# Hybrid attention block on one core: the softmax division moved to VectorE, the keys' second copies moved to DMA transfers

## The chip, the cores and the metric

The kernel runs on one core of a Trainium2 chip. The core has TensorE (PE in the profile; PEld is its weight loading), VectorE (DVE), ScalarE (ACT), GpSimd (POOL) and SyncE (SP), each with an instruction queue of its own that is worked off in order, and 16 DMA engines that serve transfers issued from the queues. The metric is the device time of one execution in microseconds (us). Before the change it is 976.67 us, the median of three runs (975.41, 976.67, 982.44).

## What is computed

One layer over 512 positions of width 2048, in float32. A modulated RMSNorm is followed by one wide input projection, then two token mixers read it: a dilated-window attention with 16 heads of 64, and a gated linear attention (GLA) with 4 heads. Both are gated, joined, projected out, added to the residual and normalised. Cut to the attention, which the change touches:

```python
s = jnp.einsum('bnqrhe,bnkrhe->bhrnqk', qb, kw) * (E ** -0.5)
s = s + bias[None, :, None, None]
s = jnp.where(mask, s, NEG_INF)
m = jnp.max(s, axis=-1, keepdims=True)
p = jnp.exp(s - m)
den = jnp.sum(p, axis=-1, keepdims=True)
o = jnp.einsum('bhrnqk,bnkrhe->bhrnqe', p / den, vw)
...
mix_w = jax.nn.softmax(jnp.stack(lses, axis=0), axis=0)
att = jnp.einsum('pbsh,pbshe->bshe', mix_w, jnp.stack(outs, axis=0))
```

The three dilation patterns share one softmax in the kernel: a row of biases per head holds the pattern multiplicities, so that one 512 by 512 score matrix per head gives the merged result.

## The kernel before, in words

**Precision.** Every large product is made of float32r matmuls of high and low parts: `three` (lines 168 to 171) multiplies high by high, low by high and high by low. Weights come in by transfers of 512 KB on SyncE's queue (`fetch`, L299) into four buffers, ScalarE rounds them to the high part (L326), VectorE subtracts to get the low part (L310).

**Units.** After a first part that computes the values and the first queries and keys (`sta`, `stb`), the projections run as units of 192 matmuls each: qk2, qk4, qk6 (queries and keys of two pairs of heads each), gk, gv0, gv1, ag0, ag1, gg0, gg1, o0 to o3. TensorE's order is the order of the code (it is scheduled by hand); the order on the other engines is set by the tile framework. Each unit takes a list of side work that is dropped in between its matmuls at given fractions of the unit (`unit`). Units qk2, qk4, qk6 and gk carry the attention of four heads each, that is 16 tiles of 128 queries by 512 keys (`attention`): 64 tiles in all. qk6 and gk carry sums as well: VectorE multiplies half matrices of 512 KB (`rawv`) with a broadcast row (`shb`) and adds them up (L698, L259).

**Queries and keys.** `qk_evict` (L549) takes a pair of heads out of PSUM at the end of a unit. For each head, 64 partitions `own` hold it and the other 64, `oth`, get a copy, so that one matmul over 128 partitions adds the query's high and low part against the same keys. The query's high part goes to `own` (ScalarE, L557), its low part to `oth` (VectorE, L558). The keys' high part `ks` is written by ScalarE twice, to `own` (L566) and to `oth` (L567); the keys' low part `kl` by VectorE twice (L568, L569).

**One tile of attention.** `score`: two matmuls of queries with `ks` and `kl` (L594, L595); VectorE adds the biases and finds the row's extreme (L598, to `p` and `st`); ScalarE takes the exponential with the row sum (L601); VectorE inverts the sum (L602, 128 by 1); GpSimd multiplies the tile by it (L603). `turn`, which stands after the next tile's `score` in TensorE's order: four transposes of the tile to PSUM (L615), ScalarE's rounded copy (L619) and VectorE's remainder (L620). `values`: eight matmuls with the values per two tiles (L629), then ScalarE and VectorE bring the output to `cat` (L632, L636).

GpSimd does nothing else until the GLA (L785) and the last projection (L1042). SyncE's queue carries the weight loads, the biases per head (L582) and the half matrices (L693).

Of the kernel before, what the change touches and what calls it, by code (L numbers as in the profile page):

```python
# [10 lines left out]
F32 = mybir.dt.float32  # L11
F32R = mybir.dt.float32r
I32 = mybir.dt.int32
AF = mybir.ActivationFunctionType
ALU = mybir.AluOpType
# [118 lines left out]
def block_kernel(ctx: ExitStack, tc: tile.TileContext, a: dict):  # L134
    nc = tc.nc
# [11 lines left out]
    def T2(name, dt=F32, parts=P):  # L147
        return t2.tile([parts, 512], dt, tag="t2", name=name)

    def B8(name, shape, dt=F32):  # L150
        return b8.tile([P] + shape, dt, tag="b8", name=name)
# [4 lines left out]
    def PA(name):  # L156
        return pp.tile([P, 512], F32, tag="pa", bufs=3, name=name)

    mm = nc.tensor.matmul
    tt = nc.vector.tensor_tensor  # L160
    stt = nc.vector.scalar_tensor_tensor
    act = nc.scalar.activation
# [335 lines left out]
    for i in range(n):  # L498
        mm_task(i)
        st, k, j = chain[i]  # L500
# [15 lines left out]
    for i in range(n, 2 * n):  # L516
        mm_task(i)
        st, k, j = chain[i]
# [30 lines left out]
    def qk_evict(p, psq, psk):  # L549

        for j in range(2):
            own = slice(64 * j, 64 * j + 64)
            oth = slice(64 - 64 * j, 128 - 64 * j)
            qs = T2(f"qs{p}{j}", F32R)
            act(qs[own], psq[own, ::-1], AF.Copy, scale=-0.125)  # L557
            stt(qs[oth], psq[own, ::-1], -0.125, qs[own].bitcast(F32),  # L558
                op0=ALU.mult, op1=ALU.subtract)
            stacks[2 * p + j] = [qs, None, None, own]  # L560
        for j in range(2):
            own = slice(64 * j, 64 * j + 64)
            oth = slice(64 - 64 * j, 128 - 64 * j)
            ks = T2(f"ks{p}{j}", F32R)
            kl = T2(f"kl{p}{j}", F32R)
            act(ks[own], psk[own], AF.Copy)  # L566
            act(ks[oth], psk[own], AF.Copy)  # L567
            tt(kl[own], psk[own], ks[own].bitcast(F32), op=ALU.subtract)  # L568
            tt(kl[oth], psk[own], ks[own].bitcast(F32), op=ALU.subtract)  # L569
            stacks[2 * p + j][1:3] = ks, kl  # L570

    cat = [None] * 4
# [1 line left out]
    def attention(pairs):  # L574

        tiles = [(2 * p + j, i) for p in pairs for j in range(2) for i in range(4)]
        gt, pt, pr_ = {}, {}, {}
        heads = [2 * p + j for p in pairs for j in range(2)]

        def g_load(h):  # L580
            g = gp.tile([P, 896], F32, tag="g", name=f"g{h}")
            nc.sync.dma_start(g, bass.AP(grow.tensor, grow.offset + h * 1024, [[1, P], [1, 896]]))  # L582
            gt[h] = g

        def score(h, i):
            def go():
                if h % 8 == 0 and i == 0:
                    cat[h // 8] = B8(f"cat{h // 8}", [4, 512])
                if i == 1 and h != heads[-1]:
                    g_load(h + 1)  # L590
                qs, ks, kl, _ = stacks[h]
                q = slice(P * i, P * i + P)
                ps = PA(f"s{h}{i}")
                mm(ps, qs[:, q], ks, start=True, stop=False)  # L594
                mm(ps, qs[:, q], kl, start=False, stop=True)  # L595
                t = T2(f"p{h}{i}")
                st = sm.tile([P, 3], F32, tag="st", name=f"st{h}{i}", bufs=6)
                nc.vector.tensor_tensor_reduce(  # L598
                    out=t, in0=ps, in1=gt[h][:, P * i:P * i + 512], op0=ALU.add, op1=ALU.min,
                    scale=1.0, scalar=3e38, accum_out=st[:, 0:1])  # L600
                act(t, t, AF.Exp, bias=st[:, 0:1], scale=-1.0, accum_out=st[:, 1:2])  # L601
                nc.vector.reciprocal(st[:, 2:3], st[:, 1:2])  # L602
                nc.gpsimd.tensor_scalar(t, t, st[:, 2:3], 1.0, op0=ALU.mult, op1=ALU.mult)  # L603
                pr_[h, i] = t
            return go

        def turn(h, i):
            def go():
                half, ii = divmod(i, 2)
                if ii == 0:  # L610
                    pt[h, half] = B8(f"pt{h}{half}", [2, 4, 256], F32R)
                t = pr_.pop((h, i))
                pk = PA(f"t{h}{i}")
                for kt in range(4):
                    nc.tensor.transpose(pk[:, kt * P:kt * P + P], t[:, kt * P:kt * P + P], ident)  # L615
                hi = pt[h, half][:, 0, :, P * ii:P * ii + P]
                lo = pt[h, half][:, 1, :, P * ii:P * ii + P]
                src = pk.rearrange("p (k q) -> p k q", k=4)
                act(hi, src, AF.Copy)  # L619
                tt(lo, src, hi.bitcast(F32), op=ALU.subtract)  # L620
            return go

        def values(h, half):
            def go():
                t = pt.pop((h, half))
                po = PA(f"o{h}{half}")
                for kt in range(4):
                    for w in range(2):
                        mm(po[:, :256], vv[h // 4][:, kt, h % 4, :], t[:, w, kt, :],  # L629
                           start=kt == 0 and w == 0, stop=kt == 3 and w == 1)  # L630
                oh = sm.tile([64, 256], F32, tag="oh", name=f"oh{h}{half}", bufs=1)
                act(oh, po[64:128, :256], AF.Copy)  # L632
                own = stacks[h][3]
                p = h // 2
                dst = cat[p // 4][own, p % 4, 256 - 256 * half:512 - 256 * half]
                tt(dst[:, ::-1], po[0:64, :256], oh, op=ALU.add)  # L636
            return go

        items = []
        n = len(tiles)  # L640
        for x in range(n + 3):
            if x < n:
                items.append(score(*tiles[x]))
            if 1 <= x <= n:
                items.append(turn(*tiles[x - 1]))
            if 2 <= x <= n + 1 and tiles[x - 2][1] % 2 == 1:
                items.append(values(tiles[x - 2][0], tiles[x - 2][1] // 2))
        g_load(heads[0])
        start, span, move0, move1, move_last = ATT_AT
        at = [start + (q + 0.5) / len(items) * span for q in range(len(items))]  # L650
        at[0] -= move0
        at[1] -= move1
        at[-1] += move_last
        return list(zip(at, items))
# [263 lines left out]
    for p in range(2):  # L918
        qk_evict(p, psb["b", 4 + 2 * p], psb["b", 5 + 2 * p])
    for n, p in (("qk2", 0), ("qk4", 2), ("qk6", 4)):  # L920
        ps = unit(n, False, attention((p, p + 1)) + ([(0.05, shift_row)] + some_sums(n) if p == 4 else []))
        for q in range(2):
            qk_evict(p + 2 + q, ps[2 * q], ps[2 * q + 1])
# [248 lines left out]
```

## Time and profile before

| | us |
|---|---|
| median of the runs, lowest, highest | 976.67, 975.41, 982.44 |
| span of the profiled execution | 976.7 |
| TensorE busy, idle in that span | 949.3, 27.4 |
| the stretch with attention, about | 200 to 478 |
| TensorE idle in that stretch | 12.3 |
| VectorE, ScalarE, GpSimd busy in that stretch | 186.1, 157.2, 46.4 |

The page gives no other time for the profiled execution than its span, which lies on the median. Its parts are: busy time per engine; the span in 40 slices; the DMA queues; the chain of work that ended last; groups of instructions by line, each with its count, busy time, mean duration and the idle time in front of it with what ended it; and the DMA transfers by line. Further views of the same trace list the waits of one engine, the busy time in chosen stretches, and the instructions in order of time (start, duration, engine, line, output and input, and in brackets the idle time before it with what ended it). The granted TensorE clock is 0.996 on average.

### The profile page before, as it was taken

The numbers are of one execution on the slowest core, as the hardware profiler recorded it, in microseconds if no ns is written. First come the engines' busy times: TensorE is split into PE (matmuls) and PEld (weight loads), VectorE is DVE, ScalarE is ACT, GpSimd is POOL, SyncE is SP. The second block draws the span as 40 slices with busy tenths as digits, with TensorE's granted clock in tenths as the row PEclk, the third lists the DMA queues.
The fourth block names the chain that finished last, engine by engine and source line by source line (L and its number), as shares of the span: only waits on it lengthen the run. The fifth ranks groups of instructions, "written<-read, shape, count | busy, mean of one in ns | idle before, by whom it ended". The sixth has DMA issues, their size and how long they took to land.

```text
span 976.7 us, 12006 instructions
## 1 busy us (share of the span) xinstructions
PE 949.3 (97%) x4522; PEld 782.3 (80%) x4522; DVE 619.8 (63%) x926; ACT 436.1 (45%) x731; POOL 77.4 (8%) x96
## 2 busy tenths in 40 slices
PE   8999999989999999999999999999999999999996
PEld 5888788878878777777777888888888888888886
DVE  7987899676666675776534647595885352436442
ACT  4542533565655655655413544363744151324221
POOL 0000000011111121111000000000010000203110
PEclk9999999999999999999999999999999999999998
DMA  9999487422223253432444434455465455345013
GB/s 328 411 413 369 158 324 274 132 99 77 93 84 101 86 192 103 127 107 91 135 169 162 130 108 142 139 170 176 130 220 181 141 173 192 106 132 171 22 43 130
DMA packets 42849, 159.69 MB, mean 163 GB/s; under 512 B 5252, under 2 KB 5796, under 8 KB 38056
## 3 DMA queue, kind: packets, MB, share of 16 engines
q1 hardware_dynamic: 42616, 158.61, 47.1%
q8 instruction: 35, 0.57, 0.2%
q10 hardware_dynamic: 176, 0.33, 0.1%
q14 instruction: 22, 0.18, 0.1%
HBM read 154.64 MB, written 4.28 MB: 163 GB/s over the span
## 4 chain that ended last, share of the span: by engine, by line
PE 76%; DVE 10%; DMA 5%; ACT 4%; issue 4%; POOL 1%; DVEq 0%; POOLq 0%; ACTq 0%
PE ps_o L170 6%; PE ps_o L169 6%; PE ps_o L171 6%; DMA rawg<-in_wg 4%; PE ps_qk L169 3%; PE sta L169 3%; PE stb L169 3%; PE ps_qk L171 3%; PE ps_qk L170 3%; PE stb L170 3%; PE sta L170 3%; PE stb L171 3%; PE sta L171 3%; PE ps_gv L171 3%; PE ps_gv L170 3%
## 5 line engine op out<-in xcount | busy, mean ns | idle before, releaser
L603 POOL TENSOR_SCALAR p<-p,st 128x512 f32<-128x512 f32 x64 | 46.4, 724 | 428.2 <-DVE st L602 412.7
L601 ACT ACTIVATE p<-p,st 128x512 f32<-128x512 f32 x64 | 46.1, 721 | 62.2 <-DVE st L598 62.1
L259 DVE CUSTOM_DVE_ANT_0 cb<-cb,sb,c_bcond 128x2048 f32<-128x2048 f32 (+1 forms) x32 | 73.4, 2293 | 0.1
L620 DVE TENSOR_TENSOR pt<-t,pt 128x512 fp32r<-128x512 f32 x64 | 44.1, 689 | 17.8 <-ACT pt L619 17.7
L615 PE MATMUL t<-c_ident,p 128*128 128x128 f32 x256 | 38.9, 274 | 10.0 <-POOL p L603 10.0
L615 PEld LDWEIGHTS t<-c_ident,p 128*128 128x128 f32 x256 | 30.9, 140 | 21.7 <-POOL p L603 14.9
L598 DVE CUSTOM_DVE_ANT_0 p<-s,g 128x512 f32<-128x512 f32 x64 | 43.6, 686 | 7.0 <-PE s L595 6.5
L619 ACT ACTIVATE pt<-t 128x512 fp32r<-128x512 f32 x64 | 37.9, 592 | 21.0 <-PE t L615 20.4
L259 DVE CUSTOM_DVE_ANT_0 rawg<-rawg,sb,gate 128x1024 f32<-128x1024 f32 x16 | 20.6, 1290 | 26.6 <-DMA rawg<-in_wg 26.6
L259 DVE CUSTOM_DVE_ANT_0 rawg<-rawg,sb,c_bcond 128x1024 f32<-128x1024 f32 x16 | 20.5, 1283 | 26.5 <-DMA rawg<-in_wg 26.5
L629 PEld LDWEIGHTS o<-pt,vv 128*128 128x128 f32 x256 | 34.2, 189 | 3.6 <-DVE pt L620 1.7
L629 PE MATMUL o<-pt,vv 128*128 128x256 f32 x256 | 35.9, 282 | 0.0
L1042 POOL TENSOR_TENSOR x<-x,fgain 128x512 f32<-128x512 f32 x12 | 20.3, 1697 | 184.6 <-ACT ysq L1032 184.6
L1032 ACT ACTIVATE ysq<-x 128x512 f32<-128x512 f32 (+1 forms) x17 | 10.3, 606 | 48.8 <-DVE x L1029 46.8
L602 DVE RECIPROCAL st<-st 128x1 f32<-128x1 f32 x64 | 10.4, 162 | 31.3 <-ACT p L601 31.2
L785 POOL TENSOR_SCALAR dc<-st,sc 128x256 f32<-128x256 f32 x16 | 10.5, 657 | 243.3 <-DVE st L782 238.4
L1028 DVE TENSOR_TENSOR y<-ps_o,sb 128x512 f32<-128x512 f32 (+1 forms) x17 | 11.1, 653 | 23.6 <-PE ps_o L171 23.6
L594 PE MATMUL s<-ks,qs 128*128 128x512 f32 x64 | 25.3, 396 | 0.2 <-DVE qs L558 0.2
L595 PE MATMUL s<-kl,qs 128*128 128x512 f32 x64 | 25.0, 390 | 0.0
L792 ACT ACTIVATE sq<-st,sc 128x256 f32<-128x256 f32 x24 | 12.2, 509 | 25.6 <-DVE st L787 13.5
L636 DVE TENSOR_TENSOR cat<-o,oh 64x256 f32<-64x256 f32 x32 | 13.3, 416 | 12.1 <-ACT oh L632 11.8
L632 ACT ACTIVATE oh<-o 64x256 f32<-64x256 f32 x32 | 12.2, 381 | 17.4 <-PE o L629 16.7
(1285 smaller groups left out, 2964.0 us busy)
## 6 DMA issues: line engine op xcount, KB each, us to landing
cb<-in_wm SPq DMA_DIRECT2D x31, 1024.0 KB, 10.0
rawg<-in_wg SPq DMA_DIRECT2D x32, 512.0 KB, 3.4
raw_o<-in_w_o SPq DMA_DIRECT2D x32, 512.0 KB, 3.5
raw_qk<-in_w_qk SPq DMA_DIRECT2D x24, 512.0 KB, 3.4
rawb<-in_w_sb SPq DMA_DIRECT2D x16, 512.0 KB, 5.8
rawv<-in_wv SPq DMA_DIRECT2D x16, 512.0 KB, 3.4
raw_gv<-in_w_gv SPq DMA_DIRECT2D x16, 512.0 KB, 3.4
raw_ag<-in_w_ag SPq DMA_DIRECT2D x16, 512.0 KB, 3.3
```

What stands on the lines that cost most here:

```text
L169: mm(ps, lh, rh, start=first, stop=False)
L170: mm(ps, ll, rh, start=False, stop=False)
L171: mm(ps, lh, rl, start=False, stop=last)
L259: nc.vector.tensor_tensor_reduce(out=w, in0=w, in1=with_, op0=ALU.mult, op1=ALU.add, scale=1.0, scalar=init, accum_out=dst)
L594: mm(ps, qs[:, q], ks, start=True, stop=False)
L598: nc.vector.tensor_tensor_reduce(out=t, in0=ps, in1=gt[h][:, P * i:P * i + 512], op0=ALU.add, op1=ALU.min, scale=1.0, scalar=3e38, accum_o ...
L601: act(t, t, AF.Exp, bias=st[:, 0:1], scale=-1.0, accum_out=st[:, 1:2])
L603: nc.gpsimd.tensor_scalar(t, t, st[:, 2:3], 1.0, op0=ALU.mult, op1=ALU.mult)
L615: nc.tensor.transpose(pk[:, kt * P:kt * P + P], t[:, kt * P:kt * P + P], ident)
L619: act(hi, src, AF.Copy)
L620: tt(lo, src, hi.bitcast(F32), op=ALU.subtract)
L629: mm(po[:, :256], vv[h // 4][:, kt, h % 4, :], t[:, w, kt, :], start=kt == 0 and w == 0, stop=kt == 3 and w == 1)
```

## The change

The division on L603 is issued on VectorE with one operation instead of on GpSimd with two (the second multiplied by 1.0). L567 and L569, which wrote the second copies of the keys' parts from PSUM on ScalarE and VectorE, become transfers from the first copy on GpSimd's queue, 64 partitions by 2 KB each. No buffer, no matmul and no position of side work is touched, and the order on TensorE and on SyncE's queue is the same row by row.

```diff
@@ qk_evict
             act(ks[own], psk[own], AF.Copy)
-            act(ks[oth], psk[own], AF.Copy)
+            nc.gpsimd.dma_start(ks[oth], ks[own])
             tt(kl[own], psk[own], ks[own].bitcast(F32), op=ALU.subtract)
-            tt(kl[oth], psk[own], ks[own].bitcast(F32), op=ALU.subtract)
+            nc.gpsimd.dma_start(kl[oth], kl[own])
             stacks[2 * p + j][1:3] = ks, kl
@@ score
                 nc.vector.reciprocal(st[:, 2:3], st[:, 1:2])
-                nc.gpsimd.tensor_scalar(t, t, st[:, 2:3], 1.0, op0=ALU.mult, op1=ALU.mult)
+                nc.vector.tensor_scalar(t, t, st[:, 2:3], None, op0=ALU.mult)
                 pr_[h, i] = t
```

How this moves the instructions stands in three places. First VectorE before the first attention tile, in unit qk2. `kl_1494` and `kl_1500` are the low keys of the second pair of heads, `qk23l` a weight's low part, `p_1551` and `p_1566` the first two tiles. Before:

```order
L568 TENSOR_TENSOR kl_1494<-stb_890,ks_1493 64x512
L569 TENSOR_TENSOR kl_1494<-stb_890,ks_1493 64x512
L310 TENSOR_TENSOR qk23l<-raw_qk_1513,qk23h 128x1024
L568 TENSOR_TENSOR kl_1500<-stb_890,ks_1499 64x512
L569 TENSOR_TENSOR kl_1500<-stb_890,ks_1499 64x512
L598 ISA p_1551,st_1552<-s_1548,g_1505 128x512
L598 ISA st_1552 128x1
L598 ISA p_1566,st_1567<-s_1563,g_1505 128x512
L598 ISA st_1567 128x1
L602 RECIPROCAL st_1552<-st_1552 128x1
L602 RECIPROCAL st_1567<-st_1567 128x1
L620 TENSOR_TENSOR pt_1587<-t_1588,pt_1587 128x4x128
```

After:

```order
L568 TENSOR_TENSOR kl_1494<-stb_890,ks_1493 64x512
L310 TENSOR_TENSOR qk23l<-raw_qk_1513,qk23h 128x1024
L568 TENSOR_TENSOR kl_1500<-stb_890,ks_1499 64x512
L598 ISA p_1551,st_1552<-s_1548,g_1505 128x512
L598 ISA st_1552 128x1
L598 ISA p_1566,st_1567<-s_1563,g_1505 128x512
L598 ISA st_1567 128x1
L602 RECIPROCAL st_1552<-st_1552 128x1
L603 TENSOR_SCALAR p_1551<-p_1551,st_1552 128x512
L602 RECIPROCAL st_1567<-st_1567 128x1
L603 TENSOR_SCALAR p_1566<-p_1566,st_1567 128x512
L620 TENSOR_TENSOR pt_1587<-t_1588,pt_1587 128x4x128
```

The second subtractions are gone from in front of the tile, and each division stands right behind its reciprocal.

Second, VectorE a little after the first tiles of unit qk6, where the first sums stand (`rawv_2818` and `rawv_2885`); `p_2911` is the unit's third tile, `pt_2897` takes the remainders of the first two. Before:

```order
L602 RECIPROCAL st_2874<-st_2874 128x1
L698 ISA rawv_2818,vbias_1468<-rawv_2818,shb 128x1024
L698 ISA vbias_1468 128x1
L620 TENSOR_TENSOR pt_2897<-t_2898,pt_2897 128x4x128
L598 ISA p_2911,st_2912<-s_2908,g_2788 128x512
L598 ISA st_2912 128x1
L259 ISA rawv_2885,vbias<-rawv_2885,shb,vbias_1468 128x1024
L259 ISA vbias 128x1
L602 RECIPROCAL st_2912<-st_2912 128x1
L310 TENSOR_TENSOR qk64l<-raw_qk_2849,qk64h 128x1024
L620 TENSOR_TENSOR pt_2897<-t_2925,pt_2897 128x4x128
```

After:

```order
L603 TENSOR_SCALAR p_2873<-p_2873,st_2874 128x512
L698 ISA rawv_2818,vbias_1468<-rawv_2818,shb 128x1024
L698 ISA vbias_1468 128x1
L259 ISA rawv_2885,vbias<-rawv_2885,shb,vbias_1468 128x1024
L259 ISA vbias 128x1
L620 TENSOR_TENSOR pt_2897<-t_2898,pt_2897 128x4x128
L598 ISA p_2911,st_2912<-s_2908,g_2788 128x512
L598 ISA st_2912 128x1
L310 TENSOR_TENSOR qk64l<-raw_qk_2849,qk64h 128x1024
L602 RECIPROCAL st_2912<-st_2912 128x1
L620 TENSOR_TENSOR pt_2897<-t_2925,pt_2897 128x4x128
L603 TENSOR_SCALAR p_2911<-p_2911,st_2912 128x512
```

The second sum has moved from behind the third tile's L598 to before it, and between that tile's reciprocal and its division the remainder of the tile before now stands.

Third, GpSimd's queue after the program's start. `ks_1475`, `kl_1476` are the keys of the first head, the others those of the next two. After the change:

```order
L567 DMA ks_1475<-ks_1475 64x512
L569 DMA kl_1476<-kl_1476 64x512
L567 DMA ks_1481<-ks_1481 64x512
L569 DMA kl_1482<-kl_1482 64x512
L567 DMA ks_1493<-ks_1493 64x512
L569 DMA kl_1494<-kl_1494 64x512
```

Where the 64 divisions stood, 32 transfers stand now, and the GLA's work (L785) follows behind the last of them.

## The prediction

> **What bounds the kernel now.** The first part of the page says which engine is full.
>
> ```profile
> PE 949.3 (97%) x4522; PEld 782.3 (80%) x4522; DVE 619.8 (63%) x926; ACT 436.1 (45%) x731; POOL 77.4 (8%) x96
> ```
>
> TensorE is busy for 949.3 of 976.7 us, in its own fixed order. The change adds and removes no matmul, so it can only move TensorE's 27.4 us of idle time. The busy time by stretch (columns: length, then busy time of PE, PEld, DVE, ACT, POOL, clock, DMA) shows how much of that lies where it acts, in units qk2, qk4, qk6 and gk.
>
> ```profile
> 200.00:261.00 61.00, 57.84 (x305) 47.94 (x305) 38.76 (x82) 34.00 (x67) 10.46 (x15) 1.00 0.26 84
> 261.00:331.00 70.00, 68.06 (x361) 56.33 (x361) 45.31 (x95) 40.62 (x79) 11.15 (x16) 1.00 0.28 88
> 331.00:402.00 71.00, 67.58 (x354) 55.22 (x353) 49.79 (x103) 39.78 (x78) 12.89 (x16) 1.00 0.42 137
> 402.00:478.00 76.00, 72.23 (x377) 59.11 (x376) 52.23 (x106) 42.78 (x83) 11.87 (x17) 1.00 0.37 118
> ```
>
> TensorE idles 3.16 + 1.94 + 3.42 + 3.77 = 12.3 us there. That is the ceiling of any gain, 1.3%. VectorE is 64% to 70% busy. What TensorE waited for (total, times, longest):
>
> ```profile
> PE t L615 <- POOL p L603: 10.0, 11, 2.9
> PE ps_qk L169 <- DVE qs L558: 1.0, 2, 0.5
> PE ps_gk L169 <- DVE qs L558: 0.5, 1, 0.5
> PE ps_qk L169 <- DVE kl L569: 0.2, 1, 0.2
> PE ps_gk L169 <- DVE kl L569: 0.2, 1, 0.2
> ```
>
> 10.0 us are transposes waiting for GpSimd's division, only 11 of 64 times. The other rows are a unit's first matmuls, which wait until VectorE has emptied a PSUM bank. In order of time the waits are of four kinds:
>
> ```profile
> 203.21 0.39 PE L595 MATMUL s<-kl,qs 128*128 128x512 f32 x1
> 204.50 0.47 PE L594 MATMUL s<-ks,qs 128*128 128x512 f32 x1 [0.22 <-DVE qs L558]
> 211.58 0.66 PE L615 MATMUL t<-c_ident,p 128*128 128x128 f32 x4 [2.94 <-POOL p L603]
> ...
> 263.83 0.66 PE L615 MATMUL t<-c_ident,p 128*128 128x128 f32 x4 [0.38 <-POOL p L603]
> ...
> 270.48 0.47 PE L169 MATMUL ps_qk<-h_hi,qk40h 128*128 128x512 f32 x1 [0.23 <-DVE kl L569]
> 272.61 0.47 PE L169 MATMUL ps_qk<-h_hi,qk40h 128*128 128x512 f32 x1 [0.52 <-DVE qs L558]
> 274.99 0.39 PE L595 MATMUL s<-kl,qs 128*128 128x512 f32 x1
> 280.71 0.66 PE L615 MATMUL t<-c_ident,p 128*128 128x128 f32 x4 [0.80 <-POOL p L603]
> ...
> 355.87 0.66 PE L615 MATMUL t<-c_ident,p 128*128 128x128 f32 x4 [0.19 <-POOL p L603]
> 371.00 0.66 PE L615 MATMUL t<-c_ident,p 128*128 128x128 f32 x4 [1.10 <-POOL p L603]
> ```
>
> At 204 to 212 and at 270 to 281 it is the start of a unit's attention, while the keys are still being evicted; at 263.83 a unit's last tile; at 355.87 and 371.00 tiles behind the sums. Why a tile is late, VectorE's rows before the first tile show, with GpSimd's first division:
>
> ```profile
> 198.22 0.68 DVE L568 TENSOR_TENSOR kl<-stb,ks 64x512 fp32r<-64x512 f32 x1 [0.53 <-ACT ks L567]
> 198.91 0.68 DVE L569 TENSOR_TENSOR kl<-stb,ks 64x512 fp32r<-64x512 f32 x1
> ...
> 204.88 0.68 DVE L568 TENSOR_TENSOR kl<-stb,ks 64x512 fp32r<-64x512 f32 x1 [0.52 <-ACT ks L567]
> 205.58 0.68 DVE L569 TENSOR_TENSOR kl<-stb,ks 64x512 fp32r<-64x512 f32 x1
> ...
> 208.99 0.69 DVE L598 CUSTOM_DVE_ANT_0 p<-s,g 128x512 f32<-128x512 f32 x1
> ...
> 210.57 0.16 DVE L602 RECIPROCAL st<-st 128x1 f32<-128x1 f32 x1 [0.27 <-ACT p L601]
> ...
> 264.60 0.68 DVE L568 TENSOR_TENSOR kl<-ps_qk,ks 64x512 fp32r<-64x512 f32 x1 [0.51 <-ACT ks L567]
> ```
>
> ```profile
> 210.83 1.40 POOL L603 TENSOR_SCALAR p<-p,st 128x512 f32<-128x512 f32 x2 [210.39 <-DVE st L602]
> ```
>
> The scores were done near 203.6, yet L598 starts at 208.99, because VectorE first works off the keys. So not the division's length but VectorE's queue sets the largest waits, and the two edits act on it in opposite directions.
>
> **The price of each edit.**
>
> ```profile
> L603 POOL TENSOR_SCALAR p<-p,st 128x512 f32<-128x512 f32 x64 | 46.4, 724 | 428.2 <-DVE st L602 412.7 <-PE ps_qk L171 5.1 <-DVE cat L636 4.4
> L569 DVE TENSOR_TENSOR kl<-ps_qk,ks 64x512 fp32r<-64x512 f32 x12 | 8.3, 689 | 0.2
> L567 ACT ACTIVATE ks<-ps_qk 64x512 fp32r<-64x512 f32 x12 | 7.1, 593 | 0.1
> ```
>
> The same operation, shape and form as the new division runs on VectorE at the end of the kernel (least, median, most ns):
>
> ```profile
> L1063 DVE TENSOR_SCALAR x<-x,rn x4: 479/480/483, 948.6 to 971.3; 128x512 f32<-128x512 f32 x4
> ```
>
> So VectorE gains 64 × 0.48 = 30.7 us and loses 16 × 0.69 = 11.0: net +19.7, from 186.1 to 205.8 us of about 272, or 76%. ScalarE loses 16 × 0.59 = 9.5. For a single tile the way from the reciprocal's end to the transposes shrinks: 0.48 and about 0.1 for two hand-overs, instead of 0.10 + 0.70 + 0.05 (reciprocal over at 210.73, GpSimd from 210.83, two divisions in 1.40, transposes at 211.58).
>
> *First entry (200 to 212).* Four second subtractions, 2.76, leave the queue before L598, and with them one of the 0.59 copies that the 0.53 and 0.52 waits stand for: L598 starts near 208.99 − 3.3 = 205.7. From L598 to the reciprocal's end it is 1.74 (210.73 − 208.99), plus 0.58 to the transposes: ready at 208.0. TensorE gets there at 211.58 − 2.94 − 0.22 = 208.4. Both waits go: −3.16. With the 2.76 alone it is ready at 208.55, and 0.15 stays.
>
> *The other three entries.* In each unit four subtractions (2.76) and four copies leave the eviction. The waits of 0.23 and 0.52 end more than 1 us earlier, and L598 of the unit's first tile comes at least 2 us earlier, against 0.80 that is missing. All go: 1.5 of L558, 0.4 of L569, and three waits of 0.80 for the division: −4.3.
>
> *Late tiles in the middle (371.00 and its like in gk).* VectorE's rows in qk6:
>
> ```profile
> 349.82 0.16 DVE L602 RECIPROCAL st<-st 128x1 f32<-128x1 f32 x1 [0.54 <-ACT p L601]
> 349.94 1.27 DVE L698 CUSTOM_DVE_ANT_0 rawv<-rawv,shb 128x1024 f32<-128x1024 f32 x1
> ...
> 352.77 1.28 DVE L259 CUSTOM_DVE_ANT_0 rawv<-rawv,shb,vbias 128x1024 f32<-128x1024 f32 x1
> ...
> 369.93 0.16 DVE L602 RECIPROCAL st<-st 128x1 f32<-128x1 f32 x1
> ```
>
> At 369.93 the reciprocal is late by what stands before it on VectorE, which stays. The division is then ready at 370.09 + 0.58 = 370.67 instead of 371.00: 0.33 twice, −0.7.
>
> *Last tiles of a unit (263.83).* The 0.42 of L636 now stands between reciprocal and division. That eats what the shorter division brings: +0.1 for all four.
>
> *A new stall in qk6.* Both sums, 1.2 each, now run before the third tile's L598, and a remainder (0.69) stands between its reciprocal and its division. The second tile's reciprocal ends at 349.98; with the entry 2.2 sooner its division ends at 348.3. From there: sums to 351.4 with 0.7 allowed for the broadcast row to land, remainder and L598 to 352.7, a weight's low part to 353.9, reciprocal, remainder and division to 355.2. TensorE, 1.5 us earlier by the unit's own waits, is there at 355.87 − 0.19 − 1.5 = 354.2. The wait grows from 0.19 to about 1.05: +0.9.
>
> *The queueing that I can't place.* 55 other divisions of 0.48 enter VectorE's queue. Most fall where it idled, as before a reciprocal:
>
> ```profile
> DVE st L602 <- ACT p L601: 31.2, 44, 0.9
> ```
>
> So the low end is 0 (a gain beyond the terms above is the last rival). At the high end a third of the 53 tiles that don't wait today come 0.48 late each, 8.5. Nearer to the low end: +0.7.
>
> *The transfers.* No row shows a transfer on GpSimd's queue. On SyncE's the nearest in size and the longest are:
>
> ```profile
> sel<-in_sel SPq DMA_DIRECT2D x1, 128.0 KB, 2.5
> rawa<-in_w_sa SPq DMA_DIRECT2D x15, 512.0 KB, 12.6
> ```
>
> The first head's low keys no longer wait for the second copy, are ready at 198.22 − 0.6 + 0.68 = 198.3 and needed at 203.21, so 4.9 us are free. In the later units they are ready by 265.3 (264.60 + 0.68) and needed at 274.99 − 0.75, so 8.9 are free; the other heads have more. At 2.5 the transfers cost nothing; at 12.6 they cost 7.7 at the first entry and 3.7 at each of three others. Two in a row on a queue of which I know nothing I put at 3 to 6, nearer to the row of the same size: +0.5, all at the first entry. Nothing else waits on GpSimd's queue before the GLA. [...]
>
> **The sum.** −3.2 − 4.3 − 0.7 + 0.1 + 0.9 + 0.7 + 0.5 = −6.0. The page's span of 976.7 lies on the median of 976.67, so no offset is needed: 970.7 us. A measurement of this kernel tells about 1% from no change, and this is 0.6%.
>
> **The rivals.**
>
> *Slow keys at the first entry only.* If a transfer takes 8 us, TensorE stands for 3.1 at L595 instead of at L615. For it speaks that the first use of a queue may be slow, against it the 2.5 of the like-sized load. Time: 970.7 − 0.5 + 3.1 = 973.3.
>
> *Transfers that outlast every window (the other side).* With T from subtraction to landing, TensorE loses (T − 4.9) + 3 × (T − 8.9) at L594 and L595. From T = 9.5 this eats the 6.5 gained; at 12.6 it is 18.8, so 989.0. Against it speaks that 12.6 belongs to loads of four times the size at the kernel's start, and in these units the DMA engines are 26% to 42% busy. [...]
>
> *VectorE becomes the limit.* If the queueing costs its upper 8.5, the entries' gain comes back as short waits of L615 for L603: 978.5. For it: 76% on average, near 80% in qk6 and gk. Against it: 53 of 64 tiles have room today.
>
> *The stalls go altogether.* If the new order also smooths qk6 and gk, up to 11 of 12.3 us go: 966.
>
> **How the numbers follow.** The forecast has 0.60 (965.5 to 974.5 by its own bounds), slow first keys 0.14, VectorE 0.13, slow transfers 0.07, all stalls gone 0.06. The range leaves out the slow transfers and the far ends: 965.5 to 980. Faster by over 1% (below 966.9): the last case and the forecast's edge, 0.10. Slower by over 1%: the slow transfers and a little of VectorE's case, 0.08. Within: 0.82.
>
> **What would show it.** Right: L615's wait of 2.94 gone, L603 on VectorE near 0.48, qk4's waits of 0.23 to 0.80 gone, a longer wait at qk6's third tile, TensorE's idle time from 200 to 472 near 6. Wrong: L594 or L595 waiting for a transfer after the first unit; L603 well above 0.48; many small waits of L615 for L603; or TensorE later than before at 478 though these waits are gone.

## The result, and the profile after

The changed kernel takes **963.60 us** (median of 4 runs, 962.26 to 965.78) beside 978.33 us for the kernel before on the same chip (4 runs, 975.41 to 982.44): a ratio of 0.985, 95% interval 0.982 to 0.989. Timed a second time it was 965.07 beside 976.16 us, ratio 0.988 (0.986 to 0.991). So it is 11 to 15 us faster where 6 were forecast, and 963.60 lies below the range of 965.5 to 980.0. The runs of the kernel before spread: of the 47 timed beside the experiments below, the 24 with a granted clock of 0.994 or more have a median of 975.1 us and the other 23 one of 979.4, and of the four behind the 978.33 two lie above 979.

The page of the changed kernel has, in its first part:

```profile
PE 943.4 (98%) x4522; PEld 781.7 (81%) x4522; DVE 636.0 (66%) x974; ACT 427.0 (44%) x715; POOL 47.2 (5%) x64
```

VectorE gained 16.2 us (19.7 were worked out), ScalarE lost 9.1 (9.5). But TensorE's busy time, with the same 4522 matmuls, fell by 5.9 us, which by the prediction it could not (in three later profiles of the kernel before it is 945.3 to 946.6, so only 2 to 3 of the 5.9 come of the change). By stretch (length, then PE, PEld, DVE, ACT, POOL, clock, DMA):

```profile
200.00:261.00 61.00, 60.58 (x325) 50.81 (x324) 46.17 (x101) 35.40 (x69) 4.07 (x8) 1.00 0.36 109
261.00:331.00 70.00, 69.60 (x371) 58.49 (x371) 51.37 (x108) 39.41 (x77) 4.59 (x10) 1.00 0.38 107
331.00:402.00 71.00, 68.55 (x360) 56.83 (x359) 55.61 (x117) 37.59 (x73) 4.07 (x8) 1.00 0.53 163
402.00:478.00 76.00, 74.00 (x385) 61.29 (x384) 52.75 (x111) 37.03 (x71) 1.53 (x3) 1.00 0.39 129
```

TensorE's idle time there is 0.42 + 0.40 + 2.45 + 2.00 = 5.3 us instead of 12.3. The waits of TensorE in the four units (total, times, longest):

```profile
PE t L615 <- DVE p L603: 4.2, 7, 0.8
PE s L594 <- DVE pt L620: 0.6, 1, 0.6
```

No wait at a unit's start is left: not 2.94, not 0.22, none of L558 and L569. What remains, in TensorE's order (first qk2's first transposes, which no longer wait; then its last tile; then qk6):

```profile
205.27 0.63 PE L615 MATMUL t<-c_ident,p 128*128 128x128 f32 x4
...
257.46 0.66 PE L615 MATMUL t<-c_ident,p 128*128 128x128 f32 x4 [0.42 <-DVE p L603]
...
343.29 0.50 PE L594 MATMUL s<-ks,qs 128*128 128x512 f32 x1 [0.58 <-DVE pt L620]
...
346.09 0.66 PE L615 MATMUL t<-c_ident,p 128*128 128x128 f32 x4 [0.69 <-DVE p L603]
...
360.88 0.66 PE L615 MATMUL t<-c_ident,p 128*128 128x128 f32 x4 [0.76 <-DVE p L603]
```

VectorE ahead of the first of these, with the keys' last subtraction, the first tile's L598, its reciprocal and its division:

```profile
202.17 0.69 DVE L568 TENSOR_TENSOR kl<-stb,ks 64x512 fp32r<-64x512 f32 x1
202.90 0.69 DVE L598 CUSTOM_DVE_ANT_0 p<-s,g 128x512 f32<-128x512 f32 x1
...
204.48 0.16 DVE L602 RECIPROCAL st<-st 128x1 f32<-128x1 f32 x1 [0.27 <-ACT p L601]
204.68 0.49 DVE L603 TENSOR_SCALAR p<-p,st 128x512 f32<-128x512 f32 x1
```

Counted from the unit's first matmul (196.87 before, 194.13 after), L598 starts 8.77 us into qk2 instead of 12.12: 3.35 earlier, where 3.3 was worked out. The transfers (median us from issue to landing):

```profile
ks<-ks POOLq DMA_DIRECT2D x16, 128.0 KB, 3.1
kl<-kl POOLq DMA_DIRECT2D x16, 128.0 KB, 2.7
```

Nothing waits for them. The longest took 4.6 us. The first head's low keys are over on VectorE at 195.67 and read at 200.48, so 4.8 us were free (4.9 forecast), in qk4 8.5 (8.9 forecast).

**Where the time went.** From a unit's first matmul to the next unit's, in us (the rest: from gv0's first matmul to the kernel's last):

| | start to qk2 | qk2 | qk4 | qk6 | gk | rest |
|---|---|---|---|---|---|---|
| before | 196.87 | 69.51 | 69.47 | 70.89 | 70.88 | 490.94 |
| after | 194.13 | 65.90 | 66.86 | 69.71 | 68.16 | 489.94 |

The four attention units save 10.1 us. The 2.7 at the start and the 1.0 in the rest come on top, in places where no changed instruction runs. Three questions were left: is the start chance, why do the units save 10.1 where the waits that went sum to 7.4 (12.16 before, 4.79 after), and why do the medians differ by more than the units do?

### The profile page after: what moved, and what is told of

Read it like the earlier page. It is cut to its first block, busy times and chain, and to the rows that moved or that the text cites. A ratio compares the mean times of both kernels' runs of the same rounds, so it can differ in the third digit from the quotient of the medians.

```text
span 962.9 us, 11960 instructions
## 1 busy us (share of the span) xinstructions
PE 943.4 (98%) x4522; PEld 781.7 (81%) x4522; DVE 636.0 (66%) x974; ACT 427.0 (44%) x715; POOL 47.2 (5%) x64
## 4 chain that ended last, share of the span: by engine, by line
PE 79%; DVE 8%; DMA 6%; ACT 3%; issue 2%; SPq 0%; POOL 0%; DVEq 0%; ACTq 0%; POOLq 0%
PE ps_o L171 6%; PE ps_o L169 6%; PE ps_o L170 6%; DMA rawg<-in_wg 4%; PE ps_qk L169 4%; PE ps_qk L170 4%; PE ps_qk L171 4%; PE stb L171 3%; PE stb L170 3%; PE stb L169 3%; PE ps_gv L171 3%; PE ps_gv L170 3%; PE ps_gv L169 3%; PE sta L170 3%; PE sta L171 3%; PE sta L169 3%
## 5 line engine op out<-in xcount | busy, mean ns | idle before, releaser
L598 DVE CUSTOM_DVE_ANT_0 p<-s,g 128x512 f32<-128x512 f32 x64 | 43.6, 686 | 5.2 <-PE s L595 4.5
L620 DVE TENSOR_TENSOR pt<-t,pt 128x512 fp32r<-128x512 f32 x64 | 43.9, 686 | 4.4 <-ACT pt L619 4.4
L629 PEld LDWEIGHTS o<-pt,vv 128*128 128x128 f32 x256 | 34.9, 189 | 2.8
L629 PE MATMUL o<-pt,vv 128*128 128x256 f32 x256 | 35.6, 282 | 0.0
L603 DVE TENSOR_SCALAR p<-p,st 128x512 f32<-128x512 f32 x64 | 31.1, 486 | 2.1
L567 POOL DMA_DIRECT2D ks<-ks x16 | 8.4, 523 | 377.4 <-DVE qs L558 194.7
L1028 DVE TENSOR_TENSOR y<-ps_o,sb 128x512 f32<-128x512 f32 (+1 forms) x17 | 11.1, 653 | 23.6 <-PE ps_o L171 23.6
L785 POOL TENSOR_SCALAR dc<-st,sc 128x256 f32<-128x256 f32 x16 | 10.4, 649 | 300.5 <-DVE st L782 295.6
L792 ACT ACTIVATE sq<-st,sc 128x256 f32<-128x256 f32 x24 | 12.2, 509 | 25.7 <-DVE st L787 14.3
L632 ACT ACTIVATE oh<-o 64x256 f32<-64x256 f32 x32 | 12.2, 382 | 16.6 <-PE o L629 15.6
```

The source lines that it names most:

```text
L598: nc.vector.tensor_tensor_reduce(out=t, in0=ps, in1=gt[h][:, P * i:P * i + 512], op0=ALU.add, op1=ALU.min, scale=1.0, scalar=3e38, accum_o ...
L603: nc.vector.tensor_scalar(t, t, st[:, 2:3], None, op0=ALU.mult)
```

## The experiments

My theory after the result had three parts. **Q**: VectorE's queue behind the keys sets the large waits, so the transfers bring the gain. **C**: a wait costs TensorE more than its shown length. **N**: the start is chance. Later came **G**: a wait of over 2 us can leave TensorE running slowly behind it.

**One part alone.** Division alone:

```diff
-                nc.gpsimd.tensor_scalar(t, t, st[:, 2:3], 1.0, op0=ALU.mult, op1=ALU.mult)
+                nc.vector.tensor_scalar(t, t, st[:, 2:3], None, op0=ALU.mult)
```

> Only the division moves to VectorE; the second copies of the keys stay on ScalarE and VectorE. Theory Q (VectorE's queue behind the keys' eviction sets the large waits, so the transfers bring most of the gain): L598 of a unit's first tile starts where it did, the wait of 2.94 before the transposes shrinks only by the shorter way through the division (0.75 becomes 0.48), the two waits of 1.10 shrink to about 0.8, and the program takes 0 to 2.5 us less than before. Rival D (the hand-over to GpSimd was the cost, the division brings most): it takes 8 us or more less than before.

975.16 beside 976.16 us, ratio 0.998 (0.996 to 1.000). Its VectorE and TensorE at the first entry, the unit beginning at 197.02:

```profile
209.14 0.69 DVE L598 CUSTOM_DVE_ANT_0 p<-s,g 128x512 f32<-128x512 f32 x1
```

```profile
PE t L615 <- issue: 2.7, 1, 2.7
```

L598 starts 12.12 us into the unit, as before, and the wait is 2.7 instead of 2.9. Of the two waits of 1.10 that were to shrink, the one in gk did (0.76); in qk6 there is one of 1.40 at an earlier tile instead. Transfers alone:

```diff
-            act(ks[oth], psk[own], AF.Copy)
+            nc.gpsimd.dma_start(ks[oth], ks[own])
...
-            tt(kl[oth], psk[own], ks[own].bitcast(F32), op=ALU.subtract)
+            nc.gpsimd.dma_start(kl[oth], kl[own])
```

> Only the second copies become transfers; the division stays on GpSimd. Theory Q: L598 of a unit's first tile starts 3 us earlier, the waits of 2.94, 0.80, 0.52 and 0.23 at the starts of the units are gone or under 0.5, the two waits of 1.10 stay, and the program takes 8 to 11 us less than before. Rival D: it takes less than 4 us less. If the transfers' descriptors and the divisions on GpSimd hinder each other, the divisions show 0.70 and more and the waits come back at the units' starts.

965.88 beside 976.16 us, ratio 0.989 (0.987 to 0.992). VectorE's L598 with the unit's start at 197.41, and TensorE's waits:

```profile
206.18 0.69 DVE L598 CUSTOM_DVE_ANT_0 p<-s,g 128x512 f32<-128x512 f32 x1
```

```profile
PE t L615 <- POOL p L603: 4.7, 7, 1.2
```

L598 is 8.77 us into the unit, just as with both edits. Q stands: the transfers bring 9.5 of the attention's 10.1 us, the division alone 1.2, and together they save 10.1, a little less than the sum of the two. The divisions on GpSimd keep to 0.70 beside the transfers, whose issue takes 0.51 to 0.53 and which land after medians of 2.8 and 2.7: no hindrance is seen.

**The start.** The changed kernel again, without an edit:

> The changed kernel once more, with a second profile. Theory N (the 2.7 us by which the first profile of the changed kernel reached unit qk2 earlier are chance, since no changed instruction had run by then): the first matmul of qk2 lies anywhere between 193 and 198, and the program's time follows it. Rival S (the start is shorter because of the change): it lies at 194.1 within 0.5 again, and that of the kernel before at 196.9 within 0.5.

And the kernel before:

> The kernel before once more, for a second profile of its start. Theory N: its first matmul of qk2 lies anywhere between 193 and 198. Rival S: at 196.9 within 0.5. By both the four units from there to gv0 take 280.7 within 1 us, as in the first profile (477.62 less 196.87).

qk2 starts at 194.24 after and at 194.59 before; over all fourteen profiles of this case it lies between 192.2 and 197.4, four of them of the kernel before (193.6, 194.1, 194.6, 196.9). N stands, and the first profile of before was a late one: the spread is there already when the wait of 2.0 us ahead of attention ends (between 104.4 and 108.5), but for up to 1.6 us that arise behind it (below). The rest behind attention varies too, from 487.8 to 491.5, the unchanged kernel alone from 488.4 to 490.9. But the second profile of before also had its four units at 283.2 us instead of 280.7, which no theory had said. qk2 took 71.06 instead of 69.51 with the same waits (and gk 1.0 more, with one wait of 1.87 instead of 0.81).

**What a wait costs.** Two places of the kernel before, TensorE's rows around the 2.94 in qk2 and around a wait of 0.52 in qk4:

```profile
208.25 0.39 PE L171 MATMUL ps_qk<-h_lo,qk21h 128*128 128x512 f32 x1
211.58 0.66 PE L615 MATMUL t<-c_ident,p 128*128 128x128 f32 x4 [2.94 <-POOL p L603]
...
271.47 0.39 PE L170 MATMUL ps_qk<-h_hi,qk40l 128*128 128x512 f32 x1
271.69 0.39 PE L171 MATMUL ps_qk<-h_lo,qk40h 128*128 128x512 f32 x1
272.61 0.47 PE L169 MATMUL ps_qk<-h_hi,qk40h 128*128 128x512 f32 x1 [0.52 <-DVE qs L558]
272.91 0.39 PE L170 MATMUL ps_qk<-h_hi,qk40l 128*128 128x512 f32 x1
```

A matmul is shown 0.39 long, but where nothing waits the next one starts 0.22 to 0.23 after it (271.47 to 271.69). The wait is counted from the end of the 0.39: 272.61 − 271.69 − 0.39 = 0.53. So the first 0.16 of this standstill are shown as busy. And the matmul behind it holds the next one up for 0.30 instead of 0.23. Together that is some 0.24, which the shown wait doesn't contain. In the table, a unit's length less its shown waits, less 0.25 for each of them:

| | qk2 | qk4 | qk6 | gk | waits shown |
|---|---|---|---|---|---|
| before | 65.2 | 66.2 | 66.7 | 66.3 | 17, 12.2 us |
| after | 65.2 | 66.2 | 66.3 | 66.1 | 8, 4.8 us |
| after, second | 65.3 | 66.2 | 66.3 | 66.1 | 9, 4.8 us |
| division alone | 65.2 | 66.1 | 66.8 | 66.2 | 17, 11.0 us |
| transfers alone | 65.5 | 66.2 | 66.3 | 66.2 | 8, 5.0 us |

In these five profiles the four are constant within 0.3 (qk6 within 0.5), whatever the kernel waits; the others follow below. The same is seen in qk4's busy time, in before, after, and the kernel with both moves below (length, then PE's busy time and matmuls):

```profile
266.38:335.85 69.47, 67.20 (x353) 55.47 (x352) 44.58 (x93) 39.76 (x76) 11.15 (x16) 1.00 0.27 88
```

```profile
260.03:326.89 66.86, 66.46 (x353) 55.88 (x352) 48.66 (x105) 37.47 (x73) 4.09 (x9) 1.00 0.37 107
```

```profile
259.02:325.24 66.22, 66.22 (x353) 55.94 (x352) 48.70 (x105) 37.33 (x73) 4.08 (x9) 1.00 0.37 108
```

353 matmuls are 67.20, 66.46 and 66.22 us "busy": of the 3.25 between the first and the last, 2.27 was shown as idle and 0.98 as busy.

**Doubled divisions**, as a test of C where there are many waits, and of VectorE's room:

```diff
                 nc.vector.tensor_scalar(t, t, st[:, 2:3], None, op0=ALU.mult)
+                nc.vector.tensor_scalar(t, t, 1.0, None, op0=ALU.mult)
```

> Behind each division stands a second pass of the same shape that multiplies by 1.0, 64 times 0.48 us more on VectorE. Theory R (VectorE has room, and the eight tiles that wait in the changed kernel are the ones without slack): these waits grow by 0.48 each, some 4 us, and a few new ones come, in all 4 to 10 us: 969 to 975. Rival V (VectorE is close to being the limit): waits at over 20 tiles, 980 and more. By both theories of what a wait costs: theory C (a wait costs TensorE its shown length and 0.25 us more, since the idle time is counted from the end of the last matmul, 0.16 after the point at which the next could have begun, and the first matmul behind it takes 0.08 longer) gives units qk2, qk4 and gk 66.2 us plus the sum of the shown waits plus 0.25 for each, within 0.2; rival I (a wait costs its length) gives 65.9 to 66.5 plus the sum of the waits alone, off by over 1 us where there are many.

977.73 beside 978.12 us, ratio 1.001 (0.999 to 1.003): all of the gain is gone. The transposes' waits (their line is L616 here, the second pass L604):

```profile
PE t L616 <- DVE p L604: 14.0, 14, 2.3
```

Fifteen waits, 14.4 us, and the units less the waits and 0.25 each are 65.1, 66.2, 67.8 and 66.1: C holds in three with the constants of the table (the 66.2 that was expected for qk2 is qk4's; qk2's is 65.2), and qk6 is 1.5 too long (below). The loss lies between what R and V gave. Eight of the waits are new and of 0.23 to 0.35 us, one to three tiles in each unit: these tiles had some 0.1 to 0.2 us left of the 0.42 that the second pass takes. VectorE's room was there, as forecast, but not much more than the change used.

**Doubled transfers**:

```diff
             nc.gpsimd.dma_start(ks[oth], ks[own])
+            nc.gpsimd.dma_start(ks[oth], ks[own])
...
             nc.gpsimd.dma_start(kl[oth], kl[own])
+            nc.gpsimd.dma_start(kl[oth], kl[own])
```

> Each of the 32 transfers is issued twice in a row, to the same place; the second of two waits for the first. In the changed kernel the first head's low keys are ready at 195.7 and read at 200.5 (4.8 us free), in the later units 258.8 and 267.4 (8.5 us free), and a transfer lands in 2.7 to 3.1 us. Theory W (the windows decide, as in the prediction): twice takes 6 to 8 us, so TensorE stands for 1 to 4 us at L594 or L595 at the first entry, and the other entries keep theirs hidden or lose under 1 us: the program takes 1 to 5 us more than the changed kernel, 966 to 970. Rival F (a busy GpSimd queue or the transfers' traffic disturbs VectorE or TensorE): operations of VectorE grow longer than 0.49 and 0.69 and the loss is spread over the units. Rival H (windows far wider than I think): no change, 965.

972.30 beside 978.12 us, ratio 0.994 (0.992 to 0.996), half of the gain lost and more than W's 966 to 970; the four units take 279.2 us instead of 270.6. TensorE's waits (L596 and L597 are the scores here):

```profile
PE s L596 <- DVE pt L622: 2.4, 1, 2.4
PE s L596 <- DMA ks<-ks: 2.3, 1, 2.3
...
PE s L597 <- DMA kl<-kl: 1.1, 3, 0.5
```

The 2.3 stand at the first entry, as the window of 4.8 us says, and at two later entries there are waits of 0.3. Less their waits qk2 and qk6 take 66.8 and 68.0, 1.6 and 1.7 more than C gives (below). The 2.4 in qk6 come another way. VectorE's row for the first sum there, in this kernel and in the changed one:

```profile
347.07 1.22 DVE L700 CUSTOM_DVE_ANT_0 rawv<-rawv,shb 128x1024 f32<-128x1024 f32 x1 [3.53 <-DMA shb<-srow]
```

```profile
340.07 1.22 DVE L698 CUSTOM_DVE_ANT_0 rawv<-rawv,shb 128x1024 f32<-128x1024 f32 x1 [1.10 <-DMA shb<-srow]
```

The broadcast row from SyncE's queue comes later beside twice the transfers (in the 21 us around that row the loads of 512 KB on that queue land after medians of 6.0 and 4.9 us instead of 4.7 and 4.2; that the transfers' traffic is the cause is a guess, not shown), and VectorE, which waits for it, keeps a tile's L620 behind it. None of the three theories had that. Already in the changed kernel VectorE stands 1.1 us for this row. The prediction had allowed 0.7, from a division that it put 0.4 later, so that it had the sums' start right.

**The slow stretch behind a long wait.** The first entry in a later profile of the kernel before, the wait again 2.94:

```profile
208.83 1.12 PE L615 MATMUL t<-c_ident,p 128*128 128x128 f32 x4 [2.94 <-POOL p L603]
209.60 0.78 PE L169 MATMUL ps_qk<-h_hi,qk21h 128*128 128x512 f32 x1
210.17 0.63 PE L170 MATMUL ps_qk<-h_hi,qk21l 128*128 128x512 f32 x1
210.60 0.63 PE L171 MATMUL ps_qk<-h_lo,qk21h 128*128 128x512 f32 x1
...
212.17 0.40 PE L170 MATMUL ps_qk<-h_hi,qk22l 128*128 128x512 f32 x1
```

Behind the wait matmuls follow each other at 0.43 instead of 0.23, for about 3 us. The same 10 us in the profile on which the prediction rests, and in this one (the column ahead of the DMA share is the granted clock):

```profile
205.00:215.00 10.00, 7.06 (x35) 5.56 (x35) 7.60 (x15) 6.07 (x12) 1.39 (x2) 1.00 0.15 54
```

```profile
205.00:215.00 10.00, 7.06 (x29) 5.54 (x29) 6.25 (x15) 4.47 (x9) 2.08 (x3) 0.83 0.16 56
```

Same waits, same busy time, but 29 matmuls instead of 35 at a clock of 0.83. The wait ends at 211.58 in the one and at 208.83 in the other; in the 10 us behind its end it is 54 matmuls at 1.00 and 47 at 0.84. Three runs went to this question, two of the kernel before:

> The kernel before, a third profile. Theory G: qk2's wait of 2.9 either leaves the unit at 69.5 with a granted clock of 1.00 behind it, as in the first profile, or it takes 71.0 with a clock near 0.83, as in the second; the other three units keep to 69.5, 70.8 and 70.9 where their waits are those of the first profile. Rival: the second profile was an accident of another kind, and qk2 takes 69.5 again or a third value.

> The kernel before, a fourth profile, with the same expectation as for the third. Two profiles that both show 69.5 would leave the frequency of the slow case at one in four; two that show 71.0 would make it three in four.

qk2 took 71.12 and 71.03, at 0.83 both times, and the other units kept to 69.5, 70.8 and, in the second, 70.8 (gk in the first is 0.5 longer, with one wait of 0.35 more). So the first profile was the exception of four: in three, the wait cost 1.5 us more. The third run makes such waits on purpose:

```diff
                 nc.vector.tensor_scalar(t, t, st[:, 2:3], None, op0=ALU.mult)
+                for _ in range(7 if (h, i) == (heads[0], 0) else 0):
+                    nc.vector.tensor_scalar(t, t, 1.0, None, op0=ALU.mult)
```

> Behind the division of the first tile of each unit VectorE makes seven passes over it that multiply by 1.0, so that TensorE waits once in each of qk2, qk4, qk6 and gk, about 3.5 us in the first and 2.7 in the others. Theory C alone: the units take their 65.2 to 66.3 plus the sum of the waits plus 0.25 for each, within 0.3, at a granted clock of 1.00: some 978 us. Theory G (a wait of over 2 us can make TensorE run slowly for some us behind it, as in the second profile of the kernel before, in the doubled transfers and in the doubled division): the units where that happens take 1.4 to 1.8 us more than that, with a granted clock under 0.95 in the 10 us behind the wait, and where it doesn't happen they keep to the sum; at least one of the four shows it: 979 to 984 us.

985.96 beside 976.79 us, ratio 1.009 (1.006 to 1.011). The waits came out as 3.37, 2.64, 4.92 and 3.66; the 4.92 and 3.66 were longer than meant. 10 us behind the first, around the end of the second, and behind the fourth:

```profile
210.00:220.00 10.00, 10.00 (x43) 8.32 (x42) 5.83 (x12) 4.75 (x9) 0.00 (x0) 0.74 0.30 100
...
280.00:290.00 10.00, 8.20 (x46) 7.03 (x47) 7.13 (x17) 4.64 (x9) 0.00 (x0) 1.00 0.26 90
...
428.00:438.00 10.00, 10.00 (x43) 8.36 (x42) 5.83 (x12) 4.48 (x8) 0.00 (x0) 0.72 0.33 110
```

The unit behind 2.64 keeps to C (66.1), the three others are 2.0 to 2.7 us above it, more than the 1.4 to 1.8 of G. G stands but for that size, and for the program's time, which it had at 979 to 984. Over all runs: none of the waits in the four units under 2 us shows the slow stretch, of ten between 2.25 and 3.0 six do (in the doubled divisions one of 2.25 does and the other doesn't), of three above 3.3 all.

A cleaner case lies ahead of attention. There every one of the fourteen profiles has the same wait of 2.04 or 2.05 us (L169 waiting for ScalarE's L392, the first row of the last view of this section), and the code behind it is the same. From its end to qk2's first matmul it takes 87.54 to 87.56 us in six profiles, with a granted clock of 1.00 in the 5 us behind the wait, and 88.71 to 89.17 in the other eight, with 0.66 or 0.67. So a wait of one and the same length leaves TensorE slow or doesn't, and where it does that costs 1.2 to 1.6 us. In the changed kernel, one of the eight, matmuls follow each other there at 0.42 to 0.43 from 106.45 to 109.01 and at 0.22 to 0.24 from 109.34. Why one wait leaves TensorE slow and another of the same length doesn't, no run shows.

**Taking away what is left.** The sums of qk6 and gk moved to later units:

```diff
-SUMS_IN = {"qk6": 4, "gk": 4, "gv0": 9, "gv1": 2, "ag0": 7, "ag1": 9, "gg0": 9}
+SUMS_IN = {"qk6": 0, "gk": 0, "gv0": 13, "gv1": 4, "ag0": 8, "ag1": 9, "gg0": 10}
```

> The eight sums that VectorE does in qk6 and gk are done in gv0 (four), gv1 (two), ag0 and gg0 instead. Theory M (what is left of waits in the middle of qk6 and gk comes from tiles behind these sums): the waits of 0.58, 0.69, 0.76 and 0.76 go, qk6 falls from 69.8 to about 67, gk from 68.1 to about 67.1, and if the later units hide the sums the program takes 3 to 4 us less than the changed kernel, 961 to 962. Rival L (the later units have no room either): the same gain in attention, given back in gv0 or gv1 as waits behind the sums, 964 to 967.

962.51 beside 978.12 us, ratio 0.984 (0.982 to 0.987); qk6 66.97, gk 67.21, each with its last tile's wait alone. M stands. The rest took 491.5, the longest of all fourteen profiles (the others 487.8 to 490.9), so something may be given back there; with one profile that stays open. A unit's last transposes three matmuls later:

```diff
-        at[-1] += move_last
+        at[-1] += move_last; at[-2] += 0.02
```

> The transposes of a unit's last tile are put three matmuls (0.68 us) later in TensorE's order. Theory T (TensorE comes to them 0.4 us too early, 0.8 in gk, because L636 and the tile's division stand one behind the other): the waits of 0.42, 0.40 and 0.41 go and that of 0.77 falls to about 0.1; by theory C that is worth 4 times 0.25 more than the 1.9 shown, 2.6 us: 962.5. Rival I (a wait costs its length): 1.9 us, 963.2. If the next unit's first evictions are late in return, nothing or a loss.

963.54 beside 978.12 us, ratio 0.986 (0.983 to 0.989), which can't be told from the changed kernel. But by units: qk2 and qk4 lost their only wait, of 0.42 and 0.40, and became 0.64 shorter each, as C says and not I. In qk6 the new order put a weight's low part (L310) between the third tile's reciprocal and its division, and its wait grew from 0.69 to 1.30; in gk a wait of 0.32 came at L629. Both moves:

> The changed kernel with the sums of qk6 and gk done in later units and with the transposes of a unit's last tile three matmuls later. Theory C (a wait costs TensorE its shown length and 0.25 us more): no wait is left in qk2, qk4 and qk6 and at most 0.4 in gk, so the four units take 65.2, 66.2, 66.3 and 66.2 to 66.8, 264.2 in all against 270.7; the later units give back the 1.6 that they gave back when the sums alone were moved; the program takes 4 to 5 us less than the changed kernel, 960. Rival I (a wait costs its length): 1.9 and 2.8 us of waits go, 3.1 net of the 1.6, 962.

**959.39** beside 976.79 us, ratio 0.982 (0.979 to 0.984). The units take 65.26, 66.22, 66.36 and 66.52, 264.4 in all where C gave 264.2, and no wait is shown in them. TensorE's longest waits are now elsewhere, the first where the second set of products begins ahead of attention, the second at the kernel's start, the third in gv0:

```profile
PE stb L169 <- ACT h_hi L392: 2.0, 1, 2.0
PE hot L200 <- DVE idle L187: 1.5, 1, 1.5
PE plr L942 <- DVE lrs L935: 1.4, 1, 1.4
```

This version beats both kernels: 17 us under before, against 11 to 15 for the change alone (each beside the kernel before, not beside each other).

## Why the prediction was wrong

The mechanism was right; the price of a wait was wrong, and two allowances came to nothing.

- **First entry.** Both waits went and L598 moved by 3.35 us. The price was wrong: −3.16 forecast; in the first two profiles qk2 became 3.6 shorter, and against the other three profiles of before 5.1 to 5.2, with the slow stretch.
- **Other three entries.** All their waits went, as forecast (−4.3). With 0.25 for each of the eight they were worth −6.4.
- **Late middle tiles.** 1.10 became 0.76 twice: right.
- **Last tiles of a unit.** +0.1 forecast. Three of the four changed by +0.03 to +0.04, that of qk4 went from 0.71 to 0.40: −0.2.
- **The new stall in qk6.** It came, as 0.69 at the tile and 0.58 at the score in front of it (0.69 and 0.24 in the second profile, with 0.29 at the values later), where 1.05 at the tile was forecast. VectorE did what was worked out: its first sum began at 340.07, where the forecast, moved to this profile's unit start, has 340.0. What was missed is that the score in front of the tile waits too, for the remainder (L620) behind the sums. With the transfers alone the stall is there as well (0.57 and 0.25), so it doesn't need the division's move.
- **Queueing, +0.7.** Nothing: no tile waits that did not wait before, but for those in qk6. The doubled divisions show that it would have begun with a few tenths more. (The "55 other divisions" should be 53: 64 less the 11 that wait. The sum doesn't use it.)
- **Late first keys, +0.5.** Nothing, with median landings of 2.7 and 3.1, and 4.6 at most, in windows of 4.8 and 8.5.
- **No offset.** A run's time lies 1.8 us above its span (964.71 and 962.9 for the first profile after, 974.77 and 973.0 for the third before). So the span of 976.7 belongs to a run of some 978.5 us, and it lay on the median of 976.67 by chance. This is not where the forecast failed: the medians of the kernel before were 976.2 to 978.3.

**The step that failed** is "The change adds and removes no matmul, so it can only move TensorE's 27.4 us of idle time", with the ceiling of 12.3 drawn from it and every wait priced at its shown length. In shown waits the terms come to −7.2 (the sum without the two allowances of 0.7 and 0.5), and 12.16 − 4.79 = 7.37 us were measured. To that come nine waits fewer at 0.25, 2.3 us, and 0.5 that the units are shorter beyond it, most in qk6 and with no cause shown: together the 10.1 of the units. The allowances for queueing and keys took 1.2 off a sum that needed nothing taken off. The slow stretch of 1.5, in three of four profiles of before, gives another 1.2 on average: 11.3, beside 11.1 between the medians of the second timing. That the 14.7 of the first timing, with four runs of each kernel, is the same gain and chance is within its interval (11 to 18 us) but not shown. The last rival, "the stalls go altogether", had nearly the right time, 966, for the wrong reason: 4.8 us of waits are still there, and only the two moves took those.

## What to carry to other kernels

Count what a wait costs from start to start: TensorE's busy time contains the tail of a matmul that the next one would have overlapped (0.16 of 0.39 us here), so "idle" is a lower bound, and a wait removed is worth its length and, here, 0.25 us. Look at long waits (over 2 us here) twice: the first profile of four hid that the one in qk2 can also nearly halve the matmul rate behind it (0.43 us from start to start instead of 0.23, for about 3 us). And where a queue was the cause, the edit that took work out of it ahead of the first use paid, and the one that shortened the link after it hardly did: the transfers alone gave 9.5 of 10.1 us.

## What the runs showed of the hardware

- A transfer of 128 KB on GpSimd's queue, within SBUF, occupies GpSimd for 0.51 us (the first for 0.72) and lands after 2.2 to 4.6 us. Beside the divisions on VectorE its medians are 3.1 and 2.7 (3.3 and 2.8 in the second profile), with the divisions on GpSimd 2.8 and 2.7, in one profile; nothing waited for it either way.
- Behind a standstill of 2.25 to 3.0 us matmuls followed each other more slowly in six of ten cases (in the third and fourth profile of the kernel before at 0.43 us instead of 0.23, for about 3 us), which cost 1.5 to 1.7 us; behind one of 2.05 us, the same in every profile, in eight of fourteen, which cost 1.2 to 1.6.
- A pass over 128×512 that multiplies by a constant alone takes VectorE 0.42 us (the second pass of the doubled divisions), with the multiplier in a column 0.49 (the changed kernel's division).
